# Gathering the rows of single expert pairs with the places stationary, and products into an unread bank in the routing's waits

## The chip, the cores and the metric

One core of a Trainium2 chip runs the whole kernel in one launch. The metric is the device time of that launch in microseconds (us). Before the change the median of three runs is 954.73 us (953.29 to 957.48).

The engines have these names here: PE is TensorE, PEld its weight loads, DVE is VectorE, ACT is ScalarE, POOL is GpSimd, and SP is SyncE, whose queue issues all the loads of weights.

## The reference, cut to what matters

The kernel computes one decoder block for 512 tokens of width 1024: attention and a state-space branch, whose merged result goes through `w_out` and is added to the residual stream x, and then a mixture of experts. Only the join of the two halves and the experts matter here:

```python
x = x + gate1[:, None, :] * (merged @ w_out[layer])
h = modulate(rms_norm(x, norm2_g[layer]), shift2, scale2)
x = x + gate2[:, None, :] * hier_moe(h, ...)
return rms_norm(x, final_g)
```

`hier_moe` picks for each token the best of 4 groups and the best 2 of the 8 experts in it. Each of the 32 experts computes `(silu(a) * g) @ w_e_out`, with a and g the halves of `h @ w_e_in`, for its tokens, weighted by the router; `w_e_in` is 1024 x 1024, `w_e_out` 512 x 1024, in float32.

## The kernel before, in words

Tokens are in four tiles of 128 (NT = 4), the width in eight blocks of 128 (KC = 8). The experts go in 16 pairs (NP = 16), each expert with 64 places for tokens (CAP), so that a pair fills 128 places. Every operand that must be exact is split in two parts of type fp32r, high and low; the normed rows h are `h2h[i]` and `h2l[i]` for token tile i.

**From w_out to the routing (lines 1208 to 1241).** The products with `w_out` (`po`, `mm3x`, L185) are made for one token tile after the other. The table `beside` says after which product steps of tile i which stages of the routing are put in PE's order: `stage_t` turns rows by transposes (`turn`, L1077), `stage_l` makes the logits and DVE's rank and choice `Ma` (L1098), `stage_h` makes h and its two parts (L1120), `stage_r` counts the places (`Rm`) and builds `P0` (L1133), and `stage_x` gathers (L1203). PE's order is the written one here; DVE and ACT are ordered by a scheduler that simulates the kernel when it is built. In `stage_r` for the last tile, the low part of the last rows (`ml`) is made right behind `P0` (L1143 to L1147).

`P0[:, i]` is a matrix of 128 tokens by 128 places with a one where a token has a place. **`stage_x(i)`** adds token tile i to the gathered and turned rows of pair 0: for each part w and each of the eight blocks k, a product of 128 columns has a block of h stationary and `P0` moving (`xg_mm`, L1153), into the banks `xg0` (4 and 5). The results come out as needed by the experts, with the width on the partitions, and two copies per bank (`halves`, L1292) bring them to `xT`.

**The pairs (lines 1454 to 1503).** In pair p, PE makes hid from `xT[p]` and w_ein (`hid_mm`, L1390), the first half of the give products of pair p-1 (`give`, `cb`, L1378, back to the tokens, with `add` on DVE), then a gather, turns the activations (`act_turned`, `xtp`, L1301), finds the places (`places`, `ix`, L1341), makes the other half of the give products and then yb with w_eout (`yb_mm`, L1397). The gather (`gather`, L1322) is made for two pairs at once in most rounds, with 256 columns moving; in round p = 13 (`NP - 3`) it is made for pair 15 alone, with 128. It uses the double bank `pair` (2 and 3) and bank 1.

SP loads the weights in pieces of 1 MB into a ring of 17 slots (`slot`, `fetch`, L1255). A piece is issued when PE has done its last product with what the slot held. The load of `gate2` (L1269) stands in SP's order behind the first half of pair 1's weights. `weights()` (L1158) computes the router's weights on DVE and ACT; it is issued after the last copies to `xT` of pair 0 (L1468).

The tail (from L1505) does the last pair with its own order, a branch for the case that an expert has more than 64 tokens (L1540), and the final norm.

Of the kernel before, what the change touches and what calls it, by code (L numbers as in the profile page):

```python
# [57 lines left out]
def hybrid_block(ctx: ExitStack, tc: tile.TileContext, x, cols, cst, ada_a, ada_b, b_rows, bc_rows, lamv, relb,  # L58
# [8 lines left out]
    def bank(i, shape=(128, 512), name=None):  # L67
        return psum.tile(list(shape), F32, tag=f"b{i}", name=name or f"bank{i}")
# [127 lines left out]
    def two(i, name):  # L196
        if i == 0:
            return [bank(0, name=name), bank(1, name=name)]
        t = pair(name=name)
        return [t[:, 0], t[:, 1]]  # L200
# [952 lines left out]
    def xg_mm(o, P, k, i, w, start):  # L1153

        TE.matmul(o, (h2h, h2l)[w][i][:, 128 * k:128 * k + 128], P[:, i].rearrange("p a b -> p (a b)"), start=start,  # L1155
                  stop=i == NT - 1 and w == 1, skip_group_check=True)

    def weights():  # L1158

        lg = La[:, :, 0:4]  # L1160

        def z3(j, n):
            return zz[:, j][:, :, None].to_broadcast([128, NT, n])

        V.tensor_reduce(zz[:, 0], lg, axis=AX.X, op=OP.max)
        tt(e4, lg, z3(0, 4), OP.subtract)
        S.activation(e4, e4, AF.Exp)
        V.tensor_reduce(zz[:, 1], e4, axis=AX.X, op=OP.add)
        ogb = oga[:, :, :, None].to_broadcast([128, NT, 4, 8])
        stt(o1.rearrange("p t (g e) -> p t g e", e=8), rk32, 0.0, ogb, OP.is_equal, OP.mult)  # L1170
        tt(o2, Ma2, o1, OP.subtract)
        for j, o in ((0, o1), (1, o2)):
            tt(Cw, La[:, :, 4:36], o, OP.mult)
            V.tensor_reduce(zz[:, 2 + j], Cw, axis=AX.X, op=OP.add)
        tt(zz[:, 4], zz[:, 3], zz[:, 2], OP.subtract)
        S.activation(zz[:, 4], zz[:, 4], AF.Exp)
        stt(zz[:, 5], zz[:, 4], 1.0, zz[:, 1], OP.add, OP.mult)
        V.reciprocal(zz[:, 6], zz[:, 5])
        tt(zz[:, 7], zz[:, 6], zz[:, 4], OP.mult)
        tt(o1, o1, z3(6, 32), OP.mult)  # L1180
        tt(o2, o2, z3(7, 32), OP.mult)
        tt(Cw, o1, o2, OP.add)
        c4 = Cw.rearrange("p t (q e) -> p t q e", e=2)
        hi = cwt[:, :, :, 0:4:2]
        V.tensor_copy(hi, c4)
        tt(cwt[:, :, :, 1:4:2], c4, f32(hi), OP.subtract)
        V.tensor_copy(cwt[:, :, :, 4:6], cstt[:, CST["tok"]:CST["tok"] + 2 * NT].rearrange("p (t b) -> p t b", b=2)[
            :, :, None, :].to_broadcast([128, NT, NE // 2, 2]))
        cnt = bank(6, (128, NE), "cnt")
        TE.matmul(cnt, obf, Msum[NT - 1], start=True, stop=True)  # L1190
        V.tensor_reduce(cf, cnt, axis=AX.X, op=OP.max)
        V.tensor_copy(ci, cf)
# [6 lines left out]
        tt(crow, crow, lps[NT], OP.add)  # L1199

    def stage_x(i):  # L1203
        for w in range(2):
            for k in range(KC):
                xg_mm(xg0[k // 4][:, k % 4], P0, k, i, w, i == w == k % 4 == 0)

    t_, l_, r_, h_, x_ = stage_t, stage_l, stage_r, stage_h, stage_x
    beside = {(0, 7): [(t_, 3)], (1, 1): [(l_, 3, 0)],
              (1, 3): [(t_, 0, T)], (1, 4): [(t_, 0)], (1, 7): [(l_, 0), (h_, 0)],  # L1210
              (2, 3): [(t_, 1, T)], (2, 4): [(t_, 1)], (2, 5): [(r_, 0)], (2, 7): [(l_, 1), (h_, 1)],
              (3, 2): [(x_, 0)], (3, 4): [(t_, 2, T)], (3, 6): [(r_, 1), (t_, 2)], (3, 10): [(l_, 2), (h_, 2)],
              (3, 12): [(t_, 3, T, 256)],
              (3, 15): [(x_, 1), (l_, 3, T, 256), (t_, 3, 768, 256), (r_, 2), (l_, 3, 768, 256), (h_, 3), (x_, 2), (r_, 3),
                        (x_, 3)]}
    with tc.manual_schedule(engines={mybir.EngineType.PE}):
        po = two(0, "po") + two(1, "po")
        for k in range(KC):
            if k % 2 == 0:
                ahead(44 + k // 2)  # L1220
            for i in range(NT):
                mm3x(po[i], mtile(k, i), unit(44 + k // 2)[k % 2], k == 0, k == KC - 1)
        for u in range(48, 52):
            unit(u)
        for i in range(NT):
            x1_part(i, 0, T, po[i])
        for i in range(NT):
            ps = bank((5, 0, 1, 0)[i], name="po2")
            n = T if i < 3 else 256
            for s_ in range(KC * T // n):  # L1230
                k, c0 = s_ % KC, n * (s_ // KC)
                if c0 and k == 0:
                    ps = bank(1, name="po2")
                mm3x(ps[:, c0:c0 + n], mtile(k, i), [w[:, c0:c0 + n] for w in unit(48 + k // 2)[k % 2]], k == 0, k == KC - 1)
                if k == KC - 1:
                    x1_part(i, T + c0, n, ps[:, c0:c0 + n])
                for f, *a in beside.get((i, s_), ()):
                    f(*a)
            if i == 0:
                xg0 = [bank(4 + q, (128, 4, 128), name="xg") for q in range(2)]  # L1240
    p1.close()


# [48 lines left out]
    def halves(dst, src_):  # L1292

        n = dst.shape[1] // 2
        last[:] = [e(dst[:, n * j:n * j + n], src_[:, n * j:n * j + n]) for j, e in enumerate((V.tensor_copy, S.copy))]
# [21 lines left out]
    def x_half(p, h):  # L1317
        held[p, h] = left.pop(0)
        xT[p, h] = p2.tile([128, 4, 128], F32, tag=held[p, h], name="xT")
        return xT[p, h]  # L1320

    def gather(ps, P, h, between=None):  # L1322

        n, per_bank = len(ps), 4 // len(ps)
        to = [x_half(p, h) for p in ps]
        for k0 in range(0, 4, per_bank):
            xg = bank(1, (128, per_bank, 128 * n), name="xg") if k0 else pair((128, 8 // n, 128 * n), name="xg")
            for kk in range(per_bank):
                for i in range(NT):
                    for w in range(2):  # L1330
                        xg_mm(xg[:, kk], P, 4 * h + k0 + kk, i, w, i == w == 0)
                if between and kk == 1 and k0 == 0:
                    between()
            for j in range(n):
                (V.tensor_copy, S.copy)[(j + k0 // per_bank) % 2](to[j][:, k0:k0 + per_bank], xg[:, :per_bank, 128 * j:128 * j + 128])  # L1335

    def places(p, P, j=0):

# [11 lines left out]
    def back(p, PT=None):  # L1350

        PT = PT or p2.tile([128, T], F32R, tag="PT", name="PT")
        ts(PT, iota, disp[p][0][:, 7:8], OP.is_equal)
        disp[p].append(PT)
# [29 lines left out]
    def give(p, y, i, q, b):  # L1384

        ps = bank(b, name="cb")
        give_mm(p, y, i, ps)
        add(i, 512 * q, ps)
# [53 lines left out]
    for i in range(RING):  # L1442
        p2r.tile([128, 2, D], F32, tag=f"r{i}", name="low")
    ctx.enter_context(tc.manual_schedule(engines={mybir.EngineType.SP, mybir.EngineType.PE}))
    gate2 = per.tile([128, D], F32, tag="gate2", name="gate2")
    fg = [per.tile([128, 512], F32, tag=a, name="fg") for a in ("P0", "rt")]

# [1 line left out]
    fetch(0)  # L1449
    fetch(1)  # L1450

    for h in range(2):
        halves(x_half(0, h), xg0[h])
    for p in range(NP - 1):
        fetch(p)
        fetch(p + 1)
        if p:
            ys = [weigh(p - 1, yb[q], q) for q in range(2)]
        hid = [bank(q, name="hid") for q in range(2)]
        for k in range(KC):  # L1460
            hid_mm(p, hid, k)
        a = act(hid)

        for i in range(NT * (p > 0)):
            give(p - 1, ys[0], i, 0, 4 + i)
        left += [held[p, h] for h in range(2)]
        if p == 0:
            with tc.issue_after(last[0].ins), tc.issue_after(last[1].ins):  # L1468
                weights()
                P = chosen(1, 2)  # L1470
            places(0, P0)
        turned_ = []

        def act_turned():
            turned_.append(act_turn(a, 0))

        if p == 0:
            gather((1, 2), P, 0, act_turned)
            gather((1, 2), P, 1)
            places(1, P, 0)  # L1480
            places(2, P, 1)
        elif p < NP - 3:
            if p % 2:
                P = chosen(p + 2, 2)
                gather((p + 2, p + 3), P, 0, act_turned)
            else:
                gather((p + 1, p + 2), P, 1, act_turned)
            places(p + 2, P, 1 - p % 2)
        elif p == NP - 3:
            P = chosen(NP - 1, 1)  # L1490
            gather((NP - 1, ), P, 0, act_turned)
            gather((NP - 1, ), P, 1)
            places(NP - 1, P)
        else:
            act_turned()
        hT_, = turned_
        for i in range(NT * (p > 0)):
            give(p - 1, ys[1], i, 1, 4 + i)
        back(p)
        yb = two(1, "yb")  # L1500
        if p < NP - 2:
            for f in range(4):
                yb_mm(p, yb, hT_, f)
# [272 lines left out]
```

## Time and profile before

| | |
|---|---|
| median of three runs | 954.73 us |
| the profiled execution | 954.63 us |
| its span, first to last instruction | 952.5 us |
| PE busy | 909.0 us, 95% |
| DVE, ACT, POOL busy | 501.5, 298.2, 7.2 us |
| mean granted PE clock | 0.968 |
| read from HBM | 265.68 MB |

The span is in one order of time for all views: rows begin with the time from the span's start. A PE row's duration includes its draining, which lies beside the next product; the price of a product is the distance of two starts. A granted clock of 1.00 is 2.4 GHz, 0.50 is 1.2 GHz. The routing runs from about 432 to 454 us, pair 0 from 454, and pair 14 ends with the yb at 905 us.

### The profile page before, as it was taken

To read this page: it belongs to the slowest core of one execution; us is meant where nothing else is said; L and a number is where in the kernel's file an instruction comes from. 1 tells how busy PE (TensorE), PEld (TensorE's weight loads), DVE (VectorE), ACT (ScalarE), POOL (GpSimd) and SP (SyncE) were. 2 spreads that over 40 slices of the span, in tenths; PEclk is the share of its full clock that TensorE was granted. 3 is DMA by queue.
4 is the path that set the end of the run, shared out by engine and by line. 5 is a ranking of instruction groups with operands and counts; after the bars stand their busy time and mean duration, and the time that the engine had idled before them with its cause. 6 is when DMAs were issued, how large, how long until landed. Compare 5 with 4: busy or idle time off the path is not lost. (4 is left out here: it accounts for less than half of the span.)

```text
span 952.5 us, 13019 instructions
## 1 busy us (share of the span) xinstructions
PE 909.0 (95%) x5028; PEld 569.9 (60%) x5028; DVE 501.5 (53%) x1249; ACT 298.2 (31%) x611; POOL 7.2 (1%) x12
## 2 busy tenths in 40 slices
PE   8997998889999999999999999999999999999985
PEld 4775765667777888779545554355553455546334
DVE  7896776656755566388315442244333343433336
ACT  3565578885544433242201010001010010100014
POOL 0000000000000000000000000000000000000002
PEclk9998998899999999998899999999999999997998
DMA  9925765512222633863799999999999999999902
GB/s 363 365 77 176 254 239 212 189 45 79 76 67 68 222 111 106 342 256 153 291 374 417 420 420 421 420 420 420 420 420 420 420 420 419 420 420 416 385 26 89
DMA packets 77589, 268.68 MB, mean 282 GB/s; under 512 B 5536, under 2 KB 11568, under 8 KB 77525
## 3 DMA queue, kind: packets, MB, share of 16 engines
q1 hardware_dynamic: 77524, 267.82, 71.6%
q8 instruction: 41, 0.67, 0.3%
q14 instruction: 24, 0.19, 0.1%
HBM read 265.68 MB, written 3.17 MB: 282 GB/s over the span
## 5 line engine op out<-in xcount | busy, mean ns | idle before, releaser
L1393 PE MATMUL hid<-w,xT 128*64 128x512 f32 x1024 | 225.7, 597 | 0.0
L1393 PEld LDWEIGHTS hid<-w,xT 128*64 128x64 f32 x1024 | 73.5, 138 | 146.8 <-issue 138.9
L1400 PE MATMUL yb<-w,sa 128*64 128x512 f32 x480 | 107.0, 598 | 0.0
L90 DVE TENSOR_TENSOR sa<-sa,hid 128x512 f32<-128x512 f32 (+1 forms) x17 | 11.1, 656 | 165.4 <-PE hid L1393 153.9
L90 DVE TENSOR_TENSOR wl<-ws,wh 128x1024 fp32r<-128x1024 f32 x52 | 63.4, 1221 | 54.8 <-ACT wh L153 44.1
L90 DVE TENSOR_TENSOR x<-x,cb 128x512 f32<-128x512 f32 (+1 forms) x132 | 80.2, 664 | 6.3 <-PE cb L1378 6.3
L153 ACT ACTIVATE wh<-ws 128x1024 fp32r<-128x1024 f32 x51 | 53.7, 1057 | 79.0 <-PE acc L180 24.8
L180 PE MATMUL acc<-hh,wh 128*128 128x512 f32 x176 | 74.1, 421 | 4.4 <-ACT wh L153 4.4
L1371 ACT CAST yh<-yf 128x512 fp32r<-128x512 f32 x29 | 17.9, 619 | 189.4 <-DVE yf L96 159.1
L1400 PEld LDWEIGHTS yb<-w,sa 128*64 128x64 f32 x480 | 33.4, 138 | 66.1 <-issue 66.1
L1155 PE MATMUL xg<-P,mh 128*128 128x256 f32 (+1 forms) x288 | 69.7, 294 | 1.5 <-DVE xT L1335 0.8
L180 PE MATMUL acc<-hl,wh 128*128 128x512 f32 x176 | 70.8, 403 | 0.0
L180 PE MATMUL acc<-hh,wl 128*128 128x512 f32 x176 | 70.6, 402 | 0.0
L1155 PE MATMUL xg<-P,ml 128*128 128x256 f32 (+1 forms) x288 | 68.7, 291 | 0.0
L1358 ACT ACTIVATE sa<-hid 128x512 f32<-128x512 f32 x15 | 9.0, 597 | 179.3 <-PE hid L1393 179.3
L96 DVE SCALAR_TENSOR_TENSOR yf<-yb,ws,gate 128x512 f32<-128x512 f32 x29 | 21.8, 751 | 82.2 <-PE yb L1400 81.8
L1155 PEld LDWEIGHTS xg<-P,mh 128*128 128x128 f32 x288 | 55.1, 201 | 2.2 <-DVE xT L1335 0.9
L1155 PEld LDWEIGHTS xg<-P,ml 128*128 128x128 f32 x288 | 55.4, 202 | 0.5
L1378 PE MATMUL cb<-yh,PT 128*128 128x512 f32 x116 | 49.3, 425 | 0.4 <-ACT yh L1371 0.3
L1378 PE MATMUL cb<-yl,PT 128*128 128x512 f32 x116 | 46.8, 404 | 2.2 <-DVE yl L90 2.0
L180 PEld LDWEIGHTS acc<-hh,wh 128*128 128x128 f32 x176 | 33.7, 191 | 14.1 <-ACT wh L153 4.6
L180 PEld LDWEIGHTS acc<-hh,wl 128*128 128x128 f32 x176 | 33.4, 190 | 9.4 <-issue 1.6
(304 smaller groups left out, 1424.0 us busy)
## 6 DMA issues: line engine op xcount, KB each, us to landing
w<-w_ein SPq DMA_DIRECT2D x128, 1024.0 KB, 13.7
w<-w_eout SPq DMA_DIRECT2D x63, 1024.0 KB, 17.4
ws<-units SPq DMA_DIRECT2D x52, 512.0 KB, 3.5
adaw<-ada_b SPq DMA_DIRECT2D x32, 512.0 KB, 4.6
ada<-ada_a SPq DMA_DIRECT2D x8, 512.0 KB, 8.2
ada<-ada_a SPq DMA_DIRECT2D x16, 256.0 KB, 7.3
X<-x SPq DMA_DIRECT2D x4, 512.0 KB, 6.3
x<-x SPq DMA_DIRECT2D x4, 512.0 KB, 4.9
```

What stands on the lines that cost most here:

```text
L90: return emit(o, lambda: (eng or V).tensor_tensor(o, a, b, op=op))
L96: return emit(o, lambda: V.scalar_tensor_tensor(o, a, s, b, op0=op0, op1=op1, **k))
L153: return (lambda: S.activation(hi, st, AF.Copy) if u else V.tensor_copy(hi, st)), lambda: tt(lo, st, f32(hi), OP.subtract)
L180: TE.matmul(o, a, b, start=start and i == 0, stop=stop and i == 2)
L1155: TE.matmul(o, (h2h, h2l)[w][i][:, 128 * k:128 * k + 128], P[:, i].rearrange("p a b -> p (a b)"), start=start, stop=i == NT - 1 and w == 1 ...
L1358: S.activation(a, hid[0], AF.Silu)
L1371: S.copy(yh, yf)
L1378: TE.matmul(ps, PT if len(y) == 2 else f32(PT), a, start=w == 0, stop=w == len(y) - 1)
L1393: m = TE.matmul(hid[q][64 * e:64 * e + 64], xT[p, k // 4][:, k % 4, 64 * e:64 * e + 64], ring[p][k][:, e, 512 * q:512 * q + 512], start=k ...
L1400: TE.matmul(yb[q][64 * e:64 * e + 64], hT_[:, f, 64 * e:64 * e + 64], ring[p][8 + f][:, e, 512 * q:512 * q + 512], start=f == 0, stop=f == ...
```

## The change

Three things change. First, the two gathers of a single pair (`stage_x` for pair 0, and the one for pair 15) take `P` as the stationary operand and move the rows of h, 512 columns at a time: 4 products per token tile instead of 16. The result then has the places on the partitions. So second, the gathered rows are copied to SBUF (`xrow0`, `xrow`) and turned by eight transposes, and the turned rows are copied to `xT` (`turn_rows`). `xrow0` has the memory of `gate2`, `xrow` that of `P`. For pair 15, `places` comes ahead of the copies, and the second half of the give products ahead of the transposes. Third, `keep(n)` puts n products of 512 bf16 columns, ones by ones, into bank 0, where nothing reads them; `beside` has 3, 2, 10 and 4 of them in the last list. Nothing else is changed; the parts of h and the sums are the same.

```diff
+    def xr_mm(ps, P, i):
+
+        for w in range(2):
+            for q in range(2):
+                TE.matmul(ps[q], P[:, i].rearrange("p a b -> p (a b)"), (h2h, h2l)[w][i][:, 512 * q:512 * q + 512],
+                          start=i == w == 0, stop=i == NT - 1 and w == 1)
+
...
     def stage_x(i):
-        for w in range(2):
-            for k in range(KC):
-                xg_mm(xg0[k // 4][:, k % 4], P0, k, i, w, i == w == k % 4 == 0)
-
-    t_, l_, r_, h_, x_ = stage_t, stage_l, stage_r, stage_h, stage_x
+        xr_mm(xr0, P0, i)
+
+    def keep(n):
+
+        ps = bank(0, name="wp")
+        for _ in range(n):
+            TE.matmul(ps, obf, obf[:, None, :].to_broadcast([128, 4, 128]), start=True, stop=True)
+
+    t_, l_, r_, h_, x_, wm = stage_t, stage_l, stage_r, stage_h, stage_x, keep
...
-              (3, 15): [(x_, 1), (l_, 3, T, 256), (t_, 3, 768, 256), (r_, 2), (l_, 3, 768, 256), (h_, 3), (x_, 2), (r_, 3),
-                        (x_, 3)]}
+              (3, 15): [(x_, 1), (wm, 3), (l_, 3, T, 256), (t_, 3, 768, 256), (r_, 2), (wm, 2), (l_, 3, 768, 256), (h_, 3), (x_, 2),
+                        (wm, 10), (r_, 3), (wm, 4), (x_, 3)]}
...
-                xg0 = [bank(4 + q, (128, 4, 128), name="xg") for q in range(2)]
+                xr0 = [bank(4 + q, name="xr") for q in range(2)]
+    xrow0 = per.tile([128, D], F32, tag="gate2", name="xrow")
...
+    def turn_rows(p, rows, b):
+
+        for h in range(2):
+            tp = bank(b[h], (128, 4, 128), "xrt")
+            for k in range(4):
+                TE.transpose(tp[:, k], rows[:, 512 * h + 128 * k:512 * h + 128 * k + 128], ident)
+            halves(x_half(p, h), tp)
...
+    for h in range(2):
+        halves(xrow0[:, 512 * h:512 * h + 512], xr0[h])
+    turn_rows(0, xrow0, (7, 6))
     gate2 = per.tile([128, D], F32, tag="gate2", name="gate2")
...
-    for h in range(2):
-        halves(x_half(0, h), xg0[h])
...
             P = chosen(NP - 1, 1)
-            gather((NP - 1, ), P, 0, act_turned)
-            gather((NP - 1, ), P, 1)
+            xr = two(1, "xr")
+            for i in range(NT):
+                xr_mm(xr, P, i)
+                if i == 1:
+                    act_turned()
             places(NP - 1, P)
+            xrow = p2.tile([128, D], F32, tag="P", name="xrow")
+            for h in range(2):
+                (V.tensor_copy, S.copy)[h](xrow[:, 512 * h:512 * h + 512], xr[h])
...
             give(p - 1, ys[1], i, 1, 4 + i)
+        if p == NP - 3:
+            turn_rows(NP - 1, xrow, (0, 1))
         back(p)
```

## Rows read from the trace of the kernel before

**Rows 1.** Busy time by stretch: length, engines (instructions), PE clock, DMA share, GB/s.
```profile
600.00:700.00 100.00, 100.00 (x516) 47.13 (x514) 36.77 (x70) 8.36 (x16) 0.00 (x0) 1.00 1.03 420
```

**Rows 2.** Waits of PE from 480 us on: total us, times, longest.
```profile
PE yq L1555 <- PEq L1540: 3.5, 1, 3.5
```

**Rows 3.** PE in time, an undisturbed pair: start, us, operation, [idle before, releaser].
```profile
652.39 0.60 PE L1301 MATMUL xtp<-colt,sa 128*128 128x128 f32 x4
652.74 0.36 PE L1155 MATMUL xg<-P,mh 128*128 128x256 f32 x1
...
654.69 0.50 PE L1341 MATMUL ix<-cwt,P 128*128 128x6 f32 x4
655.06 0.48 PE L1378 MATMUL cb<-yh,PT 128*128 128x512 f32 x1
...
657.07 7.09 PE L1400 MATMUL yb<-w,sa 128*64 128x512 f32 x32
663.99 13.90 PE L1393 MATMUL hid<-w,xT 128*64 128x512 f32 x64
```

**Rows 4.** PE in time, the routing and pair 0's hid.
```profile
432.33 1.01 PE L1155 MATMUL xg<-P,mh 128*128 128x128 f32 x8
...
434.07 0.34 PE L185 MATMUL po<-wh,mh 128*128 128x256 f32 x1
...
445.46 1.95 PE L1155 MATMUL xg<-P,mh 128*128 128x128 f32 x8
...
449.76 0.19 PE L1137 MATMUL lp<-Ma,ubf 128*128 128x32 bf16 x1 [0.65 <-DVE Ma L96]
...
450.68 1.94 PE L1155 MATMUL xg<-P,mh 128*128 128x128 f32 x8 [0.70 <-DVE P L90]
...
454.25 16.23 PE L1393 MATMUL hid<-w,xT 128*64 128x512 f32 x64
470.42 0.19 PE L1190 MATMUL cnt<-Ms,obf 128*128 128x32 bf16 x1
```

**Rows 5.** DVE in time, the routing.
```profile
435.48 0.75 DVE L96 SCALAR_TENSOR_TENSOR xg<-xg,nx,sh 128x512 f32<-128x512 f32 x1 [0.66 <-PE h2tp L1082]
...
450.45 1.28 DVE L90 TENSOR_TENSOR ml<-gate,mh 128x512 fp32r<-128x512 f32 x2
453.51 0.42 DVE L1295 COPY xT<-xg 128x256 f32<-128x256 f32 x1 [1.78 <-PE xg L1155]
```

**Rows 6.** PE in time, from the last pair's gather on.
```profile
855.32 0.22 PE L1155 MATMUL xg<-P,mh 128*128 128x128 f32 x1
...
860.20 0.33 PE L1155 MATMUL xg<-P,mh 128*128 128x128 f32 x1 [0.78 <-DVE xT L1335]
...
870.30 7.86 PE L1400 MATMUL yb<-w,sa 128*64 128x512 f32 x32
877.99 13.90 PE L1393 MATMUL hid<-w,xT 128*64 128x512 f32 x64
...
911.94 1.89 PE L1393 MATMUL hid<-w,xT 128*64 128x512 f32 x8
```

**Rows 7.** Busy time by stretch, around the falls of the clock (columns as in rows 1).
```profile
445.00:446.00 1.00, 1.00 (x7) 1.00 (x7) 0.62 (x5) 0.00 (x0) 0.00 (x0) 0.61 1.01 414
458.00:459.00 1.00, 1.00 (x4) 0.24 (x2) 0.67 (x5) 0.96 (x2) 0.00 (x0) 0.56 0.00 0
862.00:864.00 2.00, 2.00 (x11) 2.00 (x11) 0.00 (x0) 0.00 (x0) 0.00 (x0) 0.50 1.05 428
926.00:928.00 2.00, 0.00 (x0) 0.00 (x0) 0.63 (x2) 1.11 (x2) 0.00 (x0) 1.00 0.02 4
```

**Rows 8.** SP's queue in time: issues of loads.
```profile
462.41 0.44 SPq L1269 DMA_DIRECT2D gate<-mrd  x1
...
878.20 5.52 SPq L1263 DMA_DIRECT2D w<-w_ein  x4
```

## The prediction

> **What bounds the kernel now.** I read the table of busy times by stretch first. In the stretch of the experts TensorE (PE) is busy all of the time at full clock, and the DMA engines are full as well, at 420 GB/s [rows 1]. So the next question is which of the two waits for the other. PE's waits from 480 us to the end hold one long one, 3.5 us for its own branch instruction near the end [rows 2], and none for a load of weights. PE sets the time from the first expert pair to the tail, and the loads run ahead of it through a ring of 17 slots.
>
> Third view: PE in order of time in an undisturbed pair. From it come the prices at full clock. Eight give products, each with 128 stationary columns and 512 moving ones in fp32r, take 655.06 to 657.07, so 0.25 us each. Four transposes take 0.35 (652.39 to 652.74, the last still draining until 0.60 after the start), four products of `places` 0.37, the down products of a pair (yb) 6.92, the up products (hid) 13.90 [rows 3].
>
> Fourth, the same view of the routing, where PE is not the only one that waits. `stage_x(2)` begins at 445.46, and its 16 products of 128 columns last until the wait of 0.65 for `Ma`, which ends at 449.76. PE then waits 0.70 for `P`, runs `stage_x(3)` from 450.68 and starts hid of pair 0 at 454.25. That hid lasts until 470.42, or 16.2 us where 13.9 is the price at full clock [rows 3, 4]. VectorE (DVE) sets the two waits: rank, choice and `P` of the last token tile are a chain on it, with the low half of the last rows (`ml`, two pieces in 1.28 us) behind `P` [rows 5].
>
> Fifth, the gather of the last pair alone, 64 products of 128 columns. From its first product to the start of the next pair's hid is 855.32 to 877.99, 22.67 us, with a wait of 0.78 for a copy in it [rows 6].
>
> Sixth, the granted clock. It falls between 445 and 446 and returns between 458 and 459; 862 to 864 is at half (1.2 of 2.4 GHz) as well [rows 7]. Both stretches are those of the 128-column gathers. This explains the long hid of pair 0, and the yb behind the last gather, which takes 7.69 instead of 6.92 (870.30 to 877.99) [rows 3, 6].
>
> **The change, part by part, against the profiled execution** (954.63 us: span 952.5 and 2.13 around it, 0.1 under the median of 954.73).
>
> *Last pair, p = 13.* Removed are the 64 narrow products. Added are 16 products of the very form of the give products: 16 x 0.25 = 4.0. The 4 transposes of the activations stay (0.35), so do `places` (0.37) and the give products (2.01). New are 8 transposes of the gathered rows (2 x 0.35 = 0.70). Then yb at full clock, 6.92. The sum is 14.35 where there was 22.67: 8.3 us less [rows 3, 6]. Bounds: with 0.43 for a product (if these were at half clock, below twice the 0.25) it is 6.9 and some 5 are left; above, 8.6 with the 0.23 that products have between switches. Hidden: two copies of 512 columns from PSUM, which stand between `places` and the transposes. The give products (2.0 us) lie between them on PE, and DVE has four adds of 512 columns to do there. Priced as a piece of `ml`, which has that size (0.64) [rows 5], they take 2.6; if DVE makes its copy (0.64) behind them, the transposes wait 1.2 us. I take nothing, since the copy can start before the first give product is out. The four copies out of the transposes are behind yb's 6.92 and needed only by hid of the last pair. `xr` takes the double bank that yb takes next, and the copies that free it are the ones above, ahead of yb.
>
> For the price of a product, the Trainium skill (page "TensorE: Matmul & The Clock Gate", section "Back-to-back issue gap") has another figure: 131 ns per product 512 wide in a sustained stream. By it the gather would cost an estimated 2.1 us, and the time would be 1.9 lower than my sum. The rows here decide; none of them shows that rate.
>
> *Routing.* `stage_x(0)` takes 432.33 to 434.07, 1.74, and becomes 4 x 0.25 = 1.0: 0.74 less on PE [rows 3, 4]. DVE's work behind it is dense, with a wait of 0.66 for a transpose of PE before 435.48 [rows 5], so at most 0.66 of it reaches the chain on DVE. `stage_x(1)` saves the same 0.74, and the fillers (3 and 2) in the same list cost 5 x 0.25 = 1.25 (between 0, if all of it falls into waits, and 1.25): 0.5 later at worst. Together `Ma` comes between 0.5 later and 0.66 earlier; I take 0.4 earlier. `stage_x(2)` and ten fillers are 14 x 0.25 = 3.5, inside the 4.30 from 445.46 to 449.76: hidden behind DVE, and nothing if the clock is full. The last four fillers are 1.0 against the 0.92 from 449.76 to 450.68: 0.1.
>
> `stage_x(3)` is no longer held by PE. Its last product waits for the second piece of `ml`, which ends at 450.45 + 1.28 = 451.73, and takes 0.48 to its end: 452.2. Behind it there is now one round more: copy to SBUF (0.42), four transposes (0.60), copy to `xT` (0.42) [rows 3, 5]. For the second half that gives 453.65; the first half, which is all that hid needs to begin, is ahead of it: 453.2 to 453.65, taken as 453.4. With 0.4 earlier and 0.1 later hid starts at 453.1 and, at full clock, ends 13.9 later at 467.0 instead of 470.42: 3.4 less (bounds 2.7 and 4.3).
>
> *Everything else.* `xrow0` lies in the memory of `gate2`, whose load waits for the transposes of `xrow0`. That load is issued at 462.41 [rows 8], some 9 us after them, so SP is not held; if it were, the loads of pair 1 behind it would be. The fillers use bank 0, which nobody reads between. `weights()` waits for the last copy to `xT`, as before. The loads: the slots come free as PE uses them, so they move with the routing. The later 8.3 are gained against loads that are full anyway. The last rows of w_ein are issued from 878.20 on, in 5.52 us, and used from 911.94 on [rows 6, 8], which leaves 28 us from the last issue; 11.7 of these may go before PE could wait.
>
> The sum: 954.63 - 8.3 - 3.4 = 942.9.
>
> **The rivals.**
> *B, the clock falls in the routing all the same.* The fillers leave waits of up to a microsecond and the new round leaves PE nearly empty for 1.5. For it: before, the clock fell ahead of both of the waits in rows 4, 0.65 and 0.70, so it needed no long one [rows 4, 7]. Against it: between 926 and 928 PE did nothing at all and the clock stayed full [rows 7], and what went ahead of both falls are narrow products, which are gone. Then hid of pair 0 loses again the 2.3 us that it loses now, and fillers at half clock (up to 0.5 each) may push `r_3` back by 14 x 0.5 - 4.3 = 2.7. The routing then gains 1 or loses up to 3.5: 945.5 to 950, likeliest 946.5.
> The Trainium skill has such a rule, same page, section "A second HAM failure mode: psum-queue depth-cycling": an engine that idles briefly between groups of matmuls lets its clock go back and forth. The trace agrees for 445 us, and not for 926 us.
>
> *C, the wide products don't run at the price of the give products.* At 0.43 the last gather keeps about 5 of its 8.3 and the routing about 2: 947.5. Against it: the give products have the same operands' types and shapes, and run through every pair at 0.25 [rows 3].
>
> *D, slower.* One mechanism, at `r_3`: the clock is at half already when the ten fillers run, they hold `r_3` and with it `stage_x(3)`, and hid of pair 0 starts 3.5 later and finds no full clock until it ends, so 27.8 instead of 16.2. That is 3.5 + 11.6 - 8.3, so 961. It decides from the point at which more than 8.3 is lost, that is, at 5 us more of half-clock hid than before. Against it: before, the clock returned some 4.5 us after the hid had begun [rows 4, 7], with less work ahead of it.
>
> **How the numbers follow.** The forecast A (both places gain) gets 0.75, with 940 to 945 as its own range from the bounds of 2.7 to 4.3 and of 7.1 (with the wait of 1.2) to 8.6 and a microsecond between runs. B gets 0.15, C 0.06, D 0.04. The predicted time is A's, 942.9. The range takes in A and the larger part of B and C: 939.5 to 948. A measurement of this kernel can tell about 0.5% from no change, 4.8 us, so faster means under 949.9. A, nearly all of B and half of C lie there: 0.90. The rest of B and C is no change, 0.06, D is slower, 0.04.
>
> **What would show it.** Right: the clock at 1.00 from 440 to 480 and from 855 to 878 of the old times; hid of pair 0 at 13.9 us; gap from the first `xr` product of the last pair to the next hid about 14.4; fillers that end before `Ma` and `P`. The first hid should begin about a microsecond earlier than now, although there is one round more. Wrong: a half clock in the routing (B); `xr` products over 0.3 apart (C); waits of PE for `xrow` copies, or for loads of weights in the last two pairs. The gain in the routing and that in the last pair can be read separately, from the start of hid of pair 1 and from the stretch behind it.

## The result and the profile after

The changed kernel takes 940.59 us (median of four runs, 939.44 to 942.12) against 954.01 (952.95 to 957.48): a ratio of 0.9861, with a 95% interval of 0.9826 to 0.9895. Five more runs on another chip gave a ratio of 0.9852 (0.9822 to 0.9882). The profiled execution is the slowest of the four, 942.12, with a span of 939.9.

The routing, PE in order of time (start, us, operation, idle before and its releaser), answers to [rows 4]:

```profile
435.06 0.62 PE L1162 MATMUL xr<-mh,P 128*128 128x512 f32 x2
...
443.59 0.63 PE L1162 MATMUL xr<-mh,P 128*128 128x512 f32 x2
...
446.56 0.61 PE L1088 MATMUL lp<-rwt,h2T 128*128 128x36 f32 x4
...
448.01 2.33 PE L1216 MATMUL wp<-obf 128*128 128x512 bf16 x10
451.28 0.18 PE L1137 MATMUL lp<-Ma,ubf 128*128 128x32 bf16 x1 [0.94 <-DVE Ma L96]
...
451.33 1.02 PE L1216 MATMUL wp<-obf 128*128 128x512 bf16 x4
452.18 0.71 PE L1162 MATMUL xr<-mh,P 128*128 128x512 f32 x2
452.73 1.06 PE L1162 MATMUL xr<-ml,P 128*128 128x512 f32 x2
453.71 1.44 PE L1353 MATMUL xrt<-colt,xrow 128*128 128x128 f32 x8
455.08 13.95 PE L1412 MATMUL hid<-w,xT 128*64 128x512 f32 x64
468.96 0.19 PE L1197 MATMUL cnt<-Ms,obf 128*128 128x32 bf16 x1
```

The stretch begins 2.73 us later than before, since this execution came later to `stage_x(0)` (435.06 against 432.33). Read as distances: hid of pair 0 starts 20.02 after `stage_x(0)` instead of 21.92, and lasts 13.88 to the next product instead of 16.17. PE still waits 0.94 for `Ma` behind the ten fillers: these are hidden.

DVE in the same stretch, which answers to [rows 5]:

```profile
451.04 0.19 DVE L96 SCALAR_TENSOR_TENSOR Ma<-rt 128x32 bf16<-128x32 f32 x1
...
451.95 1.28 DVE L90 TENSOR_TENSOR ml<-gate,mh 128x512 fp32r<-128x512 f32 x2
453.23 0.42 DVE L1306 COPY xrow<-xr 128x256 f32<-128x256 f32 x1
...
454.59 0.42 DVE L1306 COPY xT<-xrt 128x256 f32<-128x256 f32 x1 [0.34 <-PE xrt L1353]
```

The first copy of the gathered rows follows `ml` without a gap: the work on DVE up to `ml`, not the new products on PE, sets the start of the turn.

Busy time by stretch, PE alone (length, PE busy, its products, PE clock, DMA share, GB/s), which answers to [rows 7]:

```profile
440.00:480.00 40.00, 38.67 (x236) 1.00 0.82 318
450.00:451.00 1.00, 0.34 (x2) 1.00 1.02 410
855.00:878.00 23.00, 23.00 (x114) 1.00 1.03 420
```

The clock is full in both places, also where PE works a third of the time. The last pair, PE in order of time, answers to [rows 6]:

```profile
853.87 0.63 PE L1162 MATMUL xr<-mh,P 128*128 128x512 f32 x2
...
857.56 0.63 PE L1162 MATMUL xr<-ml,P 128*128 128x512 f32 x2
858.02 0.50 PE L1360 MATMUL ix<-cwt,P 128*128 128x6 f32 x4
858.39 0.48 PE L1397 MATMUL cb<-yh,PT 128*128 128x512 f32 x1
...
860.32 1.04 PE L1353 MATMUL xrt<-colt,xrow 128*128 128x128 f32 x8
861.28 7.09 PE L1419 MATMUL yb<-w,sa 128*64 128x512 f32 x32
868.20 13.90 PE L1412 MATMUL hid<-w,xT 128*64 128x512 f32 x64
```

From 853.87 to 868.20 there is no wait. And the list of what PE waited for from 440 us on (total, times, longest; its first three lines) holds no load, though PE now runs 8 us further ahead in the last two pairs; it answers to [rows 2], whose branch is gone from the list:

```profile
PE cb L1397 <- DVE yl L90: 2.0, 2, 1.4
PE lp L1137 <- DVE Ma L96: 0.9, 1, 0.9
PE yq L1583 <- ACTq L1568: 0.8, 1, 0.8
```

The whole span, cut at starts of PE's rows, of two profiles of each kernel (the second ones are b1_before_again and a1_after_again below), in us:

| stretch | before | again | after | again |
|---|---|---|---|---|
| to stage_x(0) | 432.33 | 432.11 | 435.06 | 434.31 |
| to hid of pair 0 | 21.92 | 21.78 | 20.02 | 20.02 |
| hid of pair 0 | 16.17 | 15.95 | 13.88 | 13.88 |
| to the last gather | 384.90 | 384.88 | 384.91 | 384.90 |
| last gather to next hid | 22.67 | 22.66 | 14.33 | 14.34 |
| to the last turn (xtp) | 46.21 | 46.20 | 46.19 | 46.17 |
| to the final products (yq) | 4.13 | 4.29 | 1.42 | 1.42 |
| to the end | 24.17 | 25.83 | 24.09 | 24.16 |

Between the first profiles of each the difference is +2.73 - 4.19 + 0.01 - 8.34 - 0.02 - 2.71 - 0.08 = -12.60. Two of these terms were not forecast: the later start, and a gain of 2.71 ahead of the final products. They happen to cancel in this pair of profiles. The experiments ask which of the terms belong to which part of the change, what lowers the clock, and where the last two come from.

### The profile page after: what moved, and what is told of

The parts are those of the page before. It is cut to its first block, busy times and chain, and to the rows that moved or that the text cites. A ratio compares the mean times of both kernels' runs of the same rounds, so it can differ in the third digit from the quotient of the medians.

```text
span 939.9 us, 12904 instructions
## 1 busy us (share of the span) xinstructions
PE 898.8 (96%) x4967; PEld 556.7 (59%) x4967; DVE 501.6 (53%) x1252; ACT 300.3 (32%) x616; POOL 7.2 (1%) x12
## 5 line engine op out<-in xcount | busy, mean ns | idle before, releaser
L1412 PE MATMUL hid<-w,xT 128*64 128x512 f32 x1024 | 223.4, 593 | 0.0
L1155 PE MATMUL xg<-P,mh 128*128 128x256 f32 x224 | 54.7, 284 | 0.0
L1155 PE MATMUL xg<-P,ml 128*128 128x256 f32 x224 | 53.6, 280 | 0.0
L1155 PEld LDWEIGHTS xg<-P,ml 128*128 128x128 f32 x224 | 42.2, 188 | 0.5
L1155 PEld LDWEIGHTS xg<-P,mh 128*128 128x128 f32 x224 | 42.1, 188 | 0.5
```

The source lines that it names most:

```text
L1412: m = TE.matmul(hid[q][64 * e:64 * e + 64], xT[p, k // 4][:, k % 4, 64 * e:64 * e + 64], ring[p][k][:, e, 512 * q:512 * q + 512], start=k ...
```

## The experiments

**Each half alone.** e1_last_only is the kernel before with the last pair's part of the change and nothing else; e2_routing_only is the changed kernel with that part undone:

```diff
             P = chosen(NP - 1, 1)
-            xr = two(1, "xr")
-            for i in range(NT):
-                xr_mm(xr, P, i)
...
+            gather((NP - 1, ), P, 0, act_turned)
+            gather((NP - 1, ), P, 1)
             places(NP - 1, P)
...
-        if p == NP - 3:
-            turn_rows(NP - 1, xrow, (0, 1))
```

> Only the last pair's gather is changed; the routing is that of before. Theory (two separate gains): the stretch from the last gather's first product to the next hid goes from 22.67 to about 14.3 us, the routing keeps its half clock and its hid of 16.2 us, and the time is 8.3 us under before (about 945.7), or up to 2.7 us lower still if the short wait ahead of the final products (1.4 us in the changed kernel, 4.1 before) belongs to the last pair's part. Rival (one gain, that of the clock in the routing): the stretch gets shorter, but loads or the tail take it back, and the time stays within 3 us of before.

> Only the routing is changed (wide products, turned rows, fillers); the last pair is gathered as before. Theory: hid of pair 0 takes 13.9 us, the time from stage_x(0) to the end of that hid goes from 38.1 to 33.9, the last gather keeps its 22.7 with half clock, and the time is 4.2 under before (about 949.8), or up to 2.7 lower still if the short wait ahead of the final products belongs to this part. Rival: the routing's gain is lost in the first pairs, where the loads have gaps, and the time stays within 1.5 us of before.

Measured: e1_last_only 944.12 us, ratio 0.9873 (0.9848 to 0.9897); e2_routing_only 951.13, ratio 0.9927 (0.9899 to 0.9955). By stretch, e1 takes 14.34 from the last gather to the next hid (854.24 to 868.58), and its routing is that of before, 37.82 to the end of hid. e2 takes 33.91 for the routing and 22.67 for the last pair. So each half brings what it brings in the whole, 8.3 and 4.2, and neither rival holds. Both kernels also have 1.42 between the last turn and the final products, where before has 4.13. So that gain is in each half, and the two halves added would count it twice. (e2's final products have a further pause of 1.00 us at full clock, which the other profiles don't have; it was not followed up.)

**What lowers the clock.** e3_no_fillers is the changed kernel without its fillers:

```diff
-              (3, 15): [(x_, 1), (wm, 3), (l_, 3, T, 256), (t_, 3, 768, 256), (r_, 2), (wm, 2), (l_, 3, 768, 256), (h_, 3), (x_, 2),
-                        (wm, 10), (r_, 3), (wm, 4), (x_, 3)]}
+              (3, 15): [(x_, 1), (l_, 3, T, 256), (t_, 3, 768, 256), (r_, 2), (l_, 3, 768, 256), (h_, 3), (x_, 2),
+                        (r_, 3), (x_, 3)]}
```

e4_narrow_fillers is the kernel before with the same 19 fillers in the same places between its narrow stages.

> The changed kernel without its 19 filler products. Theory (the narrow products are what the clock fell with, not the waits): the clock stays at 1.00 through the routing, hid of pair 0 takes 13.9 to 14 us, and the time is that of the changed kernel within 1 us (about 940.6). Rival (the waits lower the clock, the fillers hold it): half clock from about the second wait on, hid of pair 0 takes 15 to 16.5 us, and the time is 2 to 3.5 us above the changed kernel (about 943.5).

> The kernel of before with the 19 fillers put between its narrow stages, and nothing else. Theory (narrow products lower the clock): the clock falls all the same near stage_x(2), fillers at half clock hold back the last stages, hid of pair 0 takes 16 us or more, and the time is up to 3 us above before (954 to 957). Rival (the waits lower it): the clock holds, hid takes 13.9, and the time is about 2 us under before (952).

e3's PE in order of time, and its clock (columns as in rows 1):

```profile
448.87 0.41 PE L1082 MATMUL h2tp<-colt,gate 128*128 128x128 f32 x2 [0.71 <-DVE Ma L96]
...
449.74 0.64 PE L1088 MATMUL lp<-rwt,h2T 128*128 128x36 f32 x4 [0.42 <-ACT h2T L1084]
...
454.49 0.19 PE L1137 MATMUL lp<-Ma,ubf 128*128 128x32 bf16 x1 [2.62 <-DVE Ma L96]
...
459.43 14.67 PE L1412 MATMUL hid<-w,xT 128*64 128x512 f32 x64
```

```profile
450.00:451.00 1.00, 1.00 (x7) 0.85 (x7) 0.88 (x4) 0.00 (x0) 0.00 (x0) 0.84 0.97 397
...
460.00:461.00 1.00, 1.00 (x4) 0.24 (x2) 1.00 (x4) 0.98 (x2) 0.00 (x0) 0.54 0.07 16
```

With wide products alone the clock fell at about 450.7, behind waits of 0.71 and 0.42 and ahead of the one of 2.62, and came back 1.5 us into hid. From `stage_x(0)` to the end of hid it takes 35.86, 1.96 more than with fillers. My theory, that it takes the narrow products to lower the clock, is false. The rival, that waits lower it, holds, though hid took 14.60, less than the 15 to 16.5 that it named. In the runs' times the loss is not to be told: 944.08, ratio 0.9863 (0.9831 to 0.9895), against 0.9861 with the fillers.

e4's PE in order of time:

```profile
447.87 1.11 PE L1155 MATMUL xg<-P,mh 128*128 128x128 f32 x8 [0.83 <-DVE P L90]
...
450.43 3.27 PE L1212 MATMUL wp<-obf 128*128 128x512 bf16 x10
...
456.58 13.95 PE L1399 MATMUL hid<-w,xT 128*64 128x512 f32 x64
```

Here the clock fell as well, at about 449 in `stage_x(2)`, a microsecond behind a wait of 0.83 that the fillers had left. It came back at about 452, while the ten fillers ran, so that hid took 13.89, but `r_3` was held until 453.54. So the theory was right in the fall and in the fillers that hold back `r_3`, and wrong in hid and in the time: the routing takes 37.22, 0.87 under before, and the run 950.42, a ratio of 0.9936 (0.9915 to 0.9956), which has the short branch in it too. Neither part of the change is enough: the wide products without the fillers lose 2.0 of the 4.2, the fillers without the wide products lose 3.3. In seven profiles with both and DVE's work as it is in the changed kernel, or less, the clock never fell in the routing (after, again, e2, e6, e7, e9, e10).

Whether narrow products alone lower it, without a wait, no run shows: each fall in the routing or the last gather lay in a wait or within 2.4 us behind one. Even with the routing of before, the narrow `stage_x(2)` ran at full clock to its end in e1, e8 and b1_before_again, and the clock fell in the wait for `Ma` behind it, or just as that began. b1, PE in order of time, and its clock (PE alone, columns as above for the changed kernel):

```profile
446.05 1.05 PE L1155 MATMUL xg<-P,ml 128*128 128x128 f32 x8
449.40 0.19 PE L1137 MATMUL lp<-Ma,ubf 128*128 128x32 bf16 x1 [2.30 <-DVE Ma L96]
```

```profile
446.00:447.00 1.00, 1.00 (x10) 1.00 1.01 414
447.00:448.00 1.00, 0.10 (x1) 0.92 1.05 434
```

How much the width counts beside the waits is not separated.

**Clock and width in the last pair.** e9_last_narrow_fillers is e2 with two fillers behind every eight narrow products:

```diff
                         xg_mm(xg[:, kk], P, 4 * h + k0 + kk, i, w, i == w == 0)
+                if n == 1:
+                    keep(2, 4)
```

> The routing of the changed kernel, the last pair's gather narrow as in before, with 2 fillers of 512 columns behind each 8 narrow products (16 in all, into bank 4). Theory (of the 8.3 us of the last pair, 5 are the half clock and 3.4 the width): the clock stays at 1.00, and the stretch to the next hid takes 64 x 0.111 + 16 x 0.22 + 9.7 (turn, places, give products, yb) + the wait, 20.3 to 21.2, less than the 22.7 without fillers although 3.5 us of work are added. Rival (the width alone): the clock falls all the same or its fall costs little, and the stretch takes 24 or more.

```profile
855.71 0.22 PE L1155 MATMUL xg<-P,mh 128*128 128x128 f32 x1
...
856.55 0.61 PE L1216 MATMUL wp<-obf 128*128 128x512 bf16 x2
...
876.36 13.90 PE L1414 MATMUL hid<-w,xT 128*64 128x512 f32 x64
```

The clock stays at 1.00, and the stretch takes 20.65, 2.0 less than before with 16 products more: as the theory had it. The fillers also shorten the wait in the gather, from 0.78 to 0.33. The time is 953.17, ratio 0.9951 (0.9932 to 0.9970). A second answer came unasked. e8_before_four (below) left the last pair as it was, and in its one profile the clock did not fall there:

```profile
854.36 0.22 PE L1155 MATMUL xg<-P,mh 128*128 128x128 f32 x1
...
872.21 3.17 PE L1399 MATMUL hid<-w,xT 128*64 128x512 f32 x14
```

That is 17.85 with the same narrow products and the same wait of 0.78. So the 8.34 are 4.82 of half clock (22.67 less 17.85) and 3.52 of width, wait and turn (17.85 less 14.33). The part of the clock is not always there: of the five profiles with the narrow gather and no fillers in it, four have 22.66 to 22.68, with the fall 1.3 to 1.7 us behind that wait, and one has 17.85. Whether that one is chance or belongs to e8's kernel is open, since e8 was profiled once.

**The short branch.** PE's branch instruction ahead of the final products, in the list of that line's instructions (queue, count, duration in ns at least/median/most, start), before and after:

```profile
L1540 PEldq COMPARE_BRANCH  x1: 3110/3110/3110, 924.9 to 924.9; - x1
```

```profile
L1568 PEldq COMPARE_BRANCH  x1: 407/407/407, 914.9 to 914.9; - x1
```

e1 to e4 all had 0.40 to 0.41. b1_before_again and a1_after_again are the two kernels word for word, profiled once more.

> The kernel of before, word for word, profiled once more. It tells whether two differences between the profiles belong to the kernels or to single executions: PE's branch instruction ahead of the final products (3.1 us in before, 0.4 in the changed kernel and in the four variants so far) and the start of stage_x(0) (432.3 in before, 435.1 in the changed kernel). Theory (the branch belongs to the layout of the instructions): 3.1 again, while the start of stage_x(0) moves by up to 4 us from run to run. Rival (chance of one execution): 0.4 here.

> The changed kernel, word for word, against before on this chip, and its profile once more. Theory: from stage_x(0) to the end of pair 0's hid 33.9 us at full clock, last gather to next hid 14.3, branch 0.4, so about 15 us of the profile's order of time under before less what the start of stage_x(0) moves: ratio 0.984 to 0.987. Rival B (the fillers hold the clock only in some executions): a half clock in the routing here, and 36 us instead of 33.9.

Before again had 3.37, after again 0.41: the branch belongs to the kernel, not to the execution. The start of `stage_x(0)` moved by only 0.22 and 0.75 in the second profiles, not by the up to 4 us that I expected. The routing and the last pair of after were the same again to 0.01 us, at full clock, as the theory had it. b1 took 953.94, ratio 0.9988 (0.9959 to 1.0018); a1 took 941.63. b1's row of the final products has another 1.7 us in it (25.83 to the end instead of 24.17). Before's row, b1's row and b1's clock (length, PE busy, its products, clock, DMA share, GB/s):

```profile
928.33 3.67 PE L1555 MATMUL yq<-w,hT 128*64 128x256 f32 x32 [3.54 <-PEq L1540]
```

```profile
927.87 5.36 PE L1555 MATMUL yq<-w,hT 128*64 128x256 f32 x32 [3.69 <-PEq L1540]
```

```profile
929.00:932.50 3.50, 3.50 (x20) 0.52 0.00 0
```

So the clock fell to half behind the branch in b1, and the same happened in e7 and e9 (5.36 and 5.25 for the row): in three of the four profiles with the long branch, before being the fourth. There the long branch costs 1.7 us more than its own length. From the last turn to the end the changed kernel is 2.79 us ahead in the first pair of profiles and 4.54 in the second.

e7_count_back gives the changed kernel as many PE products as before, 5028; e8_before_four gives the kernel before four more:

```diff
-                        (wm, 10), (r_, 3), (wm, 4), (x_, 3)]}
+                        (wm, 10), (small, 61), (r_, 3), (wm, 4), (x_, 3)]}
```

```diff
-              ... (h_, 3), (x_, 2), (r_, 3),
-                        (x_, 3)]}
+              ... (h_, 3), (x_, 2), (r_, 3),
+                        (wm, 4), (x_, 3)]}
```

> The changed kernel with 61 small products (128 columns) behind the ten fillers, so that PE has as many products and weight loads as in before, 5028. It tells what the length of PE's branch instruction hangs on. Theory (the number of instructions ahead of it): about 3 us again instead of 0.4. Rival (something else in the layout, or the code behind it): 0.4. The routing gets longer by 61 x 0.06 to 61 x 0.11 less the 0.94 of the wait, 3 to 6 us, in either case.

> The kernel of before with 4 fillers ahead of stage_x(3), and nothing else. For the same question, from the other side: if the branch hangs on the number of instructions ahead of it in coarse steps, four more leave it at about 3.1 us; if on their exact place, 0.4. The routing changes by less than 1.5 us (4 fillers at half clock are 1.7 against a wait of 0.7).

e7's and e8's branch:

```profile
L1574 PEldq COMPARE_BRANCH  x1: 3790/3790/3790, 914.3 to 914.3; - x1
```

```profile
L1546 PEldq COMPARE_BRANCH  x1: 507/507/507, 919.0 to 919.0; - x1
```

With 5028 products the changed kernel has the long branch, and with 5032 the kernel before has lost it. e9, with 5023, has it as well (3.38). The other counts, 4948, 4967, 4977, 4988, 5007, 5032 and 5047, have 0.40 to 0.51. So in these fourteen profiles its length goes with the number of PE products, with a band that holds 5023 and 5028 and neither 5007 nor 5032, and not with what the products do. What makes the band was not tried. e7's routing grew by 2.56 (33.90 to 36.46) from its 61 small products, under the 3 to 6 expected; its one run took 948.17, with the longer routing, the long branch and the half clock behind it. e8 took 946.20 in one run; its routing took 37.65, 0.44 under before, within the 1.5 expected.

**What the routing hangs on.** e6_fillers_20 has `(wm, 20)` for `(wm, 10)`:

> The changed kernel with 20 fillers instead of 10 ahead of the last count of places. Theory (fillers are free only while they end before DVE's Ma, which they do by 0.94 us): ten more at 0.22 are 2.2, so the count is held back by about 1.2, and hid of pair 0 starts 1.2 later after stage_x(0), 21.2 instead of 20.0. Rival (DVE's queue behind P sets the start of hid anyway): within 0.3 of 20.0.

Hid of pair 0 started 21.12 after `stage_x(0)` (456.83 less 435.71), 1.10 later, near the 1.2 expected: fillers are free to the end of the wait, and what goes beyond it holds back hid. The time is 942.84, ratio 0.9850 (0.9815 to 0.9885), not to be told from the changed kernel.

e5_ml_pool takes `ml` off DVE:

```diff
-            with tc.issue_after(p0.ins):
+            if True:
                 for q in range(2):
                     cs = slice(512 * q, 512 * q + 512)
-                    tt(h2l[i][:, cs], xg_[i][:, cs], f32(h2h[i][:, cs]), OP.subtract)
+                    tt(h2l[i][:, cs], xg_[i][:, cs], f32(h2h[i][:, cs]), OP.subtract, eng=G)
```

> The changed kernel with the low part of the last token tile's rows (ml) made on GpSimd as soon as its high part is there, instead of on DVE behind P. Theory (the second piece of ml holds the last product of stage_x(3), and DVE's queue holds the copies behind it): stage_x(3) runs through in about 1 us, hid of pair 0 starts 0.5 to 0.9 us earlier after stage_x(0) than the changed kernel's 20.0. Rival (the copies and turns behind it, or GpSimd beside DVE, cost as much): no earlier start, or up to 1 us later.

Its GpSimd and its DVE in order of time:

```profile
448.75 2.67 POOL L90 TENSOR_TENSOR ml<-gate,mh 128x512 fp32r<-128x512 f32 x2 [415.62 <-ACT mh L1129]
```

```profile
448.88 2.57 DVE L90 TENSOR_TENSOR gt<-rt 128x256 bf16<-128x256 f32 x2
```

The two subtractions on GpSimd take 2.67, and DVE's `gt` beside them takes 2.57 instead of the 0.51 of the changed kernel; the two end together. PE then waits 2.96 for `Ma`, the clock falls at about 454.7, and hid starts 22.76 after `stage_x(0)`, 2.74 later than in the changed kernel. The rival was right and even too mild. The time is 943.56, ratio 0.9859 (0.9825 to 0.9894).

e10_rank_first puts rank and choice of the last tile ahead of the two pieces that finish its rows, on DVE:

```diff
+        with tc.issue_after(ma_[i].ins) if i == NT - 1 else ExitStack():
             for q in range(2):
                 cs = slice(512 * q, 512 * q + 512)
                 stt(h2f[:, cs], h2f[:, cs], n_(i, 7), sh2[q], OP.mult, OP.add)
```

> The changed kernel with DVE's order changed for the last token tile: rank and choice (Ma) ahead of the two pieces that finish its rows, instead of behind them. Theory (the sum of DVE's work sets the start of hid, not the order, but DVE now has work while PE counts the places): Ma 1.3 us earlier after stage_x(0), the wait of PE ahead of it gone, hid of pair 0 starts 0.3 to 0.6 earlier than the changed kernel's 20.0 us after stage_x(0). The time is then equal to the changed kernel's within what can be told. Rival (the start of hid hangs on Ma): 1.3 earlier.

`Ma` came 1.19 earlier after `stage_x(0)` (449.88 less 435.09, against 15.98), PE's wait for it was gone, one of 0.59 for ACT's high part of the rows (`mh`) came ahead of `stage_x(3)`, and hid started 19.85 after `stage_x(0)`, 0.17 earlier: less than expected, since the sum of DVE's work stands ahead of the copies in either order. At 939.85, ratio 0.9838 (0.9804 to 0.9872), it is the lowest of all, but its interval overlaps with the changed kernel's by far: no version was found that is shown to beat it.

## Why the prediction was right

The forecast was 942.9 with a range of 939.5 to 948; the measured median is 940.59. The sum of its steps, 11.7, stands against 12.53 in the two stretches that it priced (8.34 and 4.19). That the profiled executions too are 12.5 apart (954.63 and 942.12) is luck: two terms that it did not price, 2.71 less and 2.73 more, cancel there.

*The last pair* was forecast at 14.35 and took 14.33. Its terms: the wide products 3.80 (853.87 to 858.02 less 0.35 for the turn) against 4.0; the eight new transposes 0.96 (860.32 to 861.28) against 0.70; the give products 1.93 against 2.01; so the terms are off by up to 0.26 and cancel. The copies cost nothing, as taken. e1 shows the gain alone and e9 and e8 what it is made of. That the width and not only the clock would count was in the step; how much of it is the clock, 4.82, was not, and this part is missing where the clock doesn't fall, as in e8.

*The routing* was forecast at 3.4 and gave 4.19. (That lies within the stated bounds of 2.7 and 4.3, but these don't follow from the step: its own terms, the start of `Ma`, 453.2 to 453.65 for the first half, and 0 to 0.1 for the last fillers, give 2.3 to 4.0.) Hid at full clock was right to 0.02, and it began 1.90 earlier after `stage_x(0)`, where the sum had 1.15. The term that was mis-sized is the start of `Ma`: taken as 0.4 earlier, with at most 0.66 from DVE's one wait, it came 1.21 earlier after `stage_x(0)` (16.22 against 17.43). The step took DVE to be the pace of that stretch with one gap. DVE's rows of before have three more waits for PE behind it:

```profile
444.08 0.19 DVE L90 TENSOR_TENSOR rt<-rt,lp 128x36 f32<-128x36 f32 x1 [0.28 <-PE lp L1088]
...
444.57 0.19 DVE L96 SCALAR_TENSOR_TENSOR Rm<-Ma,lp 128x32 f32<-128x32 bf16 x1 [0.22 <-PE lp L1139]
...
445.69 0.19 DVE L90 TENSOR_TENSOR rt<-rt,lp 128x36 f32<-128x36 f32 x1 [0.34 <-PE lp L1088]
```

With the 0.66 they are 1.50 us up to `Ma`; after, one of 0.35 is left. And 0.82 of `stage_x(0)` and 0.80 of `stage_x(1)` were saved on PE, and PE's second part of the logits of the last tile came 1.07 earlier after `stage_x(0)` (446.56 less 435.06, against 444.90 less 432.33), although five fillers went ahead of it. So PE set more of the pace there than the step allowed, though in before PE waited for DVE as well:

```profile
444.90 0.75 PE L1088 MATMUL lp<-rwt,h2T 128*128 128x36 f32 x4 [0.37 <-DVE nx L96]
```

From `Ma` to hid it took 3.80 against the 3.74 of the sum, with the whole new round in it. The ten fillers were hidden, as the step says, and e6 shows where that ends.

*Rival B* did not come in the changed kernel, but e3 shows that it was close: without fillers the clock falls between the waits. What the prediction held against B, that PE did nothing from 926 to 928 and the clock stayed full [rows 7], was true of that one execution and no protection: behind the same pause the clock fell in b1, e7 and e9. *Rival C*: the products ran at 0.23. *Rival D*: e4 has its first half, fillers at half clock that hold back `r_3`, but in it the clock is back before hid.

*Not in the forecast* was the branch, 2.71 between these profiles. I had read it [rows 2] and taken it to stay. It was the luck of an instruction count, and it hid that the start of the routing came 2.73 later. What that later start is stays open: eight of the nine profiles of kernels with the changed routing come to `stage_x(0)` at 434.3 to 438.2, e7's at 431.9, and all five with the old routing at 431.5 to 433.3, though PE, DVE and ACT have the same instructions in the same order up to there in the traces. Between after and before the difference arises between 63 and 211 us. PE's waits for loads of the conditioning's weights lie there, but they don't sort the profiles: 3.8 in after, but 2.5 in b1, which came early, and 0.7 in e2, which came late. No run here was made to settle it, so it is not excluded that the change costs these 2 to 3 us.

## What to carry to other kernels

In a gather by products with a one-hot matrix, try the wide operand as the moving one: here two more copies and a turn (0.96 on PE) were cheap for it where PE had other work beside them. Check what the clock does behind short products and short waits: here it fell behind waits with wide products too, and with narrow products where fillers had left a wait. Filler products in the waits are free as long as the wait's row still shows something left. When a few microseconds appear in a stretch that the change doesn't touch, profile both kernels a second time, and move the instruction count, before giving them to the change.

## What was not expected of the hardware

The duration of PE's branch, 0.4 to 0.5 or 3.1 to 3.8 us, goes with the number of PE products: 61 unread products put the long one into the changed kernel, four took it out of the kernel before. The clock does not do the same in every execution: it fell in the last pair's narrow gather in four of five profiles, and behind the long branch in three of four. And beside two subtractions on GpSimd (2.67 for two pieces of 512 columns) an instruction pair of DVE took 2.57 instead of 0.51.
